# S5 matmuls in blocks of one array division, GLU in the S5 operand's token order, and a norm broadcast in two one-pass matmuls

## The chip, the cores and the metric

The kernel runs on one core of a Trainium2 chip. The metric is device time in microseconds (us): the median of several executions of the same program. Beside it stands one profiled execution, whose trace gives the start, the length and the waits of every instruction. PE is the matrix engine (TensorE), PEld its weight loads, DVE the vector engine, ACT the scalar engine, POOL the general one, and SPq and ACTq are the queues on which SyncE and ACT issue DMAs.

## The reference, cut to what matters

One decoder layer on 1056 tokens (a prompt of 1024 and 8 samples of 4), all in float32:

```
n = rmsnorm(h, g_in)
z_a, xbc, dt_raw, z_b, u_b = split(n @ w_in)
ya = ssd_branch(z_a, xbc, dt_raw, ...)       # conv, SiLU, chunked SSD scan, * SiLU(z_a), grouped norm
# s5_branch: 64 groups of 16 channels, each drives a complex diagonal state of 64
bu = einsum(u, bb);  x = scan(ab, bu)        # x_t = ab * x_(t-1) + bu_t
y = Re(einsum(x, c)) + s5_d * u
g = gelu(y)
y = g * sigmoid(g @ glu_w + glu_b)           # GLU
yb = y * silu(z_b)
h = h + concat(ya, yb) @ w_out
h = h + (p @ w_ple_proj) * sigmoid(rmsnorm(h, g_ple) @ w_ple_gate)
y_out = rmsnorm(h, g_final)
```

## The kernel before, in words

Every activation lies with channels on the 128 partitions and the 1056 tokens along a row. A float32 operand of a large product is split into a high and a low part of a one-pass type (`n_h`/`n_l`, `wh`/`wl`, `g_h`/`g_l`, `yb_h`/`yb_l`), and the product is taken as high·high + low·high + high·low. That is `dense` (L164, matmuls on L173): for a tile of 128 weight rows it goes through three chunks of 352 tokens, and in each through k = 0..7, three matmuls of 352 columns for each k, into one PSUM tile `psd`. Such dense tiles run through the whole kernel and make up most of its work: projections `u`, `z_b`, `z_a` and `xbc` (moving `n_h`/`n_l`), then GLU (moving `g_h`/`g_l`), the half of the output product that reads the S5 branch (WOB, moving `yb_h`/`yb_l`), the half that reads the SSD branch (WOA, moving `ya_h`/`ya_l`), and the gate.

The order of instructions on each engine is not written out by hand. The program is built under a scheduler that simulates a timeline and picks, on each engine, what comes next. So small matmuls of the S5 and SSD parts stand between dense matmuls of whatever weight tile is running. Buffers come from pools: 28 rows of one token row each, three PSUM tiles for `psd`, two of a pool A (`vr`, `vi`, `kp`, `nsp`, `xt`, `cb`) and three of a pool B (`wp`, `yp`, `nrb`, `yd`, `yo`, `st`).

The stages, in order of time:

- **First norm and the p projection.** A row's sum of squares is taken over partitions by small matmuls with a column of ones (`rstd_tok`, `nsp` L190), its inverse root is worked out on DVE in tiny tiles of 88 tokens x 12 (`nv`, `ny`, `nt`), and `rstd_bcast` (`nrb` L208) spreads it over the 128 partitions: four float32 matmuls per chunk, with the column `ny` broadcast as weights and an identity matrix as moving operand.
- **u projection with the S5 coefficients.** 16 calls of `s5_coef_batch`, one for four S5 groups. Each works out powers of the state matrix on DVE, then eight matmuls `kp` (L450, 64 rows by 32 columns of the array each), which ACT and DVE put into `ks`, and four transposes `wp` (L471, the whole array), copied into `wo`. Results go to DRAM tiles `kd`, `md` and `od`.
- **z_b and xbc projections with the S5 batches.** 16 calls of `s5_batch`, again four groups each. A batch loads `u8`, `mm` and `om` from DRAM; eight matmuls `vr`/`vi` (L642, 128 rows by 64 columns of the array) make the drive; DVE runs the scan and writes the states `sst`; eight matmuls `yp<-sst,om` (L688, 64 rows by 128 columns) and four `yp<-u,mm` (L684, the whole array) make y; ACT applies gelu and a DMA writes `gd`. `z_tile` (L597) makes z·(1+tanh(z/2)) out of a dense tile and stores it in `zb_d` or `za_d`.
- **SSD scan with the rest of z_a.** 16 units. Each needs a decay tile `ab`, loaded by a broadcasting DMA from `acs_d`, then eight relus, exp and a mask.
- **GLU.** `g_tile` loads gelu(y) from `gd` in its own order (step s of 8, then block c of 128 tokens) and splits it into `g_h` and `g_l`, written in token order. The eight GLU tiles follow; their evacuation loads `zb_d` as `gzl`, multiplies, and splits into `yb_h`/`yb_l`. `za_apply` multiplies the SSD output by `za_d` and sums its squares (`ysq`) on POOL. `ya_norm` (norm over 512 channels) follows GLU tiles 3 and 7.
- **WOB, WOA, gate and last norm.** WOB adds x and stores in `hp_d`; WOA adds `hp_d`; the gate stage multiplies; a last norm gives the output.

The loop that places the S5 batches among the other projections is this:

```
MID = "b0 c0 dt x0 z x1 z x2 x3 z b1 c1 z x4 x5 z x6 x7".split()
for nm in MID:
    ...                      # one dense tile: dt_tile(), z_next() or conv_tile(...)
    if nb < 16:
        s5_batch(nb)
        nb += 1
```

Of the kernel before, what the change touches and what calls it, by code (L numbers as in the profile page):

```python
# [7 lines left out]
F32 = mybir.dt.float32  # L8
F32R = mybir.dt.float32r
# [15 lines left out]
CW = 352  # L25
EPS = 1e-6
# [4 lines left out]
C_ID, C_CAUS, C_ONE, C_SMASK, C_BM, C_E8, C_I32, C_SAME, C_E16, C_N = 0, 128, 256, 384, 416, 424, 488, 520, 552, 568  # L31
# [3 lines left out]
def hymba_ssd_s5_kernel(  # L35
# [141 lines left out]

    nw_p = pool("nw", bufs=2)
# [4 lines left out]
    def rstd_tok(chunks, n, eps=EPS):  # L183
# [17 lines left out]
        return y  # L201

    def rstd_bcast(y):

        qt = y.shape[0]
# [30 lines left out]
    dma(out=cs, in_=cst)  # L236
    dma(out=vc, in_=vecs)
    dma(out=raws[1], in_=wall[M_PP + 1])
# [174 lines left out]
    def s5_coef_batch(b):  # L413
        cf2, P, Z = cfc["p2"], cfc["P"], cfc["Z"]
        g0, g1, j0 = GB * b, GB * b + GB, 2 * b
        if b % 4 == 0:
# [26 lines left out]
            in_=op[:, :, :, 1:9].rearrange("p j r k h -> p (j r) (k h)"))  # L443
        kp = psa("kp")[:, 0:128]
        for j in range(2):
            for ri in range(2):
                for q in range(2):
                    g, hq = 2 * j + q, slice(64 * q, 64 * q + 64)
                    o = 128 * ri + 32 * (b % 4) + 16 * j
                    PE.matmul(out=kp[32 * g:32 * g + 32], lhsT=cfc["zf"][hq, o:o + 32],  # L450
                              rhs=op[hq, j, ri, 0:8].rearrange("p k h -> p (k h)"), start=(ri == 0), stop=(ri == 1),
                              tile_position=(64 * q, 32 * g))
# [170 lines left out]
    def s5_batch(b):  # L623
# [15 lines left out]
        for g in range(NB):  # L639
            q, j = g % 2, g // 2  # L640
            for ri, v in ((0, vrv), (1, viv)):
                PE.matmul(out=v[64 * q:64 * q + 64, j], lhsT=wv[:, 2 * j + ri, 64 * q:64 * q + 64], rhs=u8[:, g, 8:144],  # L642
                          start=True, stop=True)
# [36 lines left out]
        yp = [psb("yp")[:, 0:136 * NJ].rearrange("p (j c) -> p j c", c=136) for _ in range(2)]  # L680
        for j in range(NJ):
            for q in range(2):
                g = 2 * j + q
                PE.matmul(out=yp[q][:, j], lhsT=tm[:, g], rhs=u8[:, g, 0:136], start=True, stop=False)  # L684
            for ri in range(2):
                for q in range(2):
                    hq = slice(64 * q, 64 * q + 64)
                    PE.matmul(out=yp[q][:, j], lhsT=om[hq, j, ri], rhs=sst[hq, ri, j, 0:136], start=False, stop=(ri == 1))  # L688
# [145 lines left out]
    def ya_norm(g):  # L834

        rt = rstd_tok([[ysq[c]] for c in range(3)], 512, 4 * EPS)
        for c in range(3):
            rs = rstd_bcast(rt[:, 4 * c:4 * c + 4])
# [59 lines left out]
    for nm in MID:  # L898
# [270 lines left out]
```

## Time and profile before

| | |
|---|---|
| median of three executions | 1076.1 us (1072.94 to 1078.46) |
| profiled execution: its own time | 1074.75 us |
| profiled execution: span, first to last instruction | 1072.8 us |
| mean granted PE clock | 0.988 |
| PE busy | 1036.2 us, 97% of the span, 6948 instructions |
| PEld busy | 964.9 us, 90% |
| DVE busy | 737.7 us, 69% |
| ACT busy | 425.4 us, 40% |
| POOL busy | 166.6 us, 16% |

Busy time is the union of an engine's instructions. PE's records overlap, since matmuls are pipelined: a matmul that is listed with 0.32 us starts some 0.16 us after the one before it, so it is the distance from start to start that tells what a matmul takes. The span is shorter than the execution's own time by 1.95 us, which lie ahead of the first and behind the last instruction. The granted clock is below 1 in four short stretches, 39.6 to 46.5, 234.2 to 237.6, 776.9 to 780.3 and from 1060.2 us on.

### The profile page before, as it was taken

What the parts mean: (1) busy time and instruction counts of PE and PEld (TensorE: products, weight loads), DVE (VectorE), ACT (ScalarE), POOL (GpSimd) and SP (SyncE); (2) the same over time, 40 slices, a digit from 0 to 9 for tenths busy, and PEclk for the clock granted to TensorE, in tenths of its full rate; (3) what the DMA queues carried; (4) which work ended last, traced back from release to release, by engine and by line L of the source; (5) the groups of instructions that cost most, each with busy time, mean ns of one, the idle gap of its engine ahead of it and who ended that gap; (6) DMA issues with size and microseconds to landing.
All of it is one profiled execution on the core that took longest, in us unless ns stands there. A gap on an engine that the chain in (4) does not pass through costs nothing.

```text
span 1072.8 us, 18551 instructions
## 1 busy us (share of the span) xinstructions
PE 1036.2 (97%) x6948; PEld 964.9 (90%) x6948; DVE 737.7 (69%) x1676; ACT 425.4 (40%) x861; POOL 166.6 (16%) x225
## 2 busy tenths in 40 slices
PE   7999999999999999999999997999999999999995
PEld 7899888889889999998878885899999999999995
DVE  5789989676888687545667579889862234445676
ACT  7533222444444334348644455443521023323321
POOL 0600000000000000021333223031300002221221
PEclk9899999999999999999999999999999999999997
DMA  9524577643444343343446656544444422321332
GB/s 319 184 83 139 167 226 226 192 148 105 136 162 164 111 163 109 105 143 101 166 177 209 199 157 177 161 136 124 126 136 151 139 98 87 107 97 62 115 108 101
DMA packets 120825, 156.02 MB, mean 145 GB/s; under 512 B 15776, under 2 KB 96800, under 8 KB 120736
## 3 DMA queue, kind: packets, MB, share of 16 engines
q1 hardware_dynamic: 91712, 135.31, 39.8%
q10 hardware_dynamic: 29024, 19.54, 5.8%
q8 instruction: 54, 0.88, 0.3%
q14 instruction: 35, 0.29, 0.1%
HBM read 108.34 MB, written 50.67 MB: 148 GB/s over the span
## 4 chain that ended last, share of the span: by engine, by line
PE 44%; DVE 4%; DMA 3%; ACT 2%; issue 2%; POOL 0%; SPq 0%; DVEq 0%; ACTq 0%; POOLq 0%
PE psd L173 37%; DMA ab<-acs_d 1%; PE nrb L208 1%; PE yd L712 1%; DVE g_l L73 1%; ACT ab L70 1%; PE yo L761 1%; PE st L764 1%; DMA gr<-gd 1%; PE nsp L190 1%; PE yq L812 1%; DMA ee<-eac_d 1%; PE xt L750 0%; ACT wh L70 0%; DVE x L73 0%
## 5 line engine op out<-in xcount | busy, mean ns | idle before, releaser
L173 PE MATMUL psd<-n_h,wh 128*128 128x352 f32 x864 | 285.9, 331 | 2.5 <-DVE zt L85 2.4
L173 PE MATMUL psd<-n_l,wh 128*128 128x352 f32 x864 | 284.9, 330 | 0.0
L173 PE MATMUL psd<-n_h,wl 128*128 128x352 f32 x864 | 282.3, 327 | 0.0
L173 PEld LDWEIGHTS psd<-n_h,wh 128*128 128x128 f32 x864 | 164.3, 190 | 11.8 <-issue 4.8
L173 PEld LDWEIGHTS psd<-n_l,wh 128*128 128x128 f32 x864 | 164.5, 190 | 2.6 <-issue 1.8
L173 PEld LDWEIGHTS psd<-n_h,wl 128*128 128x128 f32 x864 | 164.0, 190 | 2.7 <-issue 1.8
L73 DVE TENSOR_TENSOR wl<-wr,wh 128x1024 fp32r<-128x1024 f32 (+1 forms) x64 | 78.4, 1225 | 72.9 <-ACT wh L70 70.6
L70 ACT ACTIVATE wh<-wr 128x1024 fp32r<-128x1024 f32 (+1 forms) x65 | 67.0, 1031 | 145.6 <-PE psd L173 130.6
L173 PE MATMUL psd<-g_l,wh 128*128 128x352 f32 x192 | 62.6, 326 | 6.4 <-DVE g_l L73 6.4
L173 PE MATMUL psd<-g_h,wh 128*128 128x352 f32 x192 | 61.8, 328 | 3.2 <-ACT g_h L70 3.1
L173 PE MATMUL psd<-yb_l,wh 128*128 128x352 f32 x192 | 62.8, 327 | 0.0
L173 PE MATMUL psd<-yb_h,wl 128*128 128x352 f32 x192 | 62.5, 325 | 0.0
L173 PE MATMUL psd<-yb_h,wh 128*128 128x352 f32 x192 | 62.4, 326 | 0.0
L173 PE MATMUL psd<-ya_l,wh 128*128 128x352 f32 x192 | 61.8, 322 | 0.0
L173 PE MATMUL psd<-ya_h,wh 128*128 128x352 f32 x192 | 61.8, 322 | 0.0
L173 PE MATMUL psd<-g_h,wl 128*128 128x352 f32 x192 | 61.8, 322 | 0.0
L173 PE MATMUL psd<-ya_h,wl 128*128 128x352 f32 x192 | 61.8, 322 | 0.0
L70 ACT ACTIVATE ab<-ab,tok 128x128 f32<-128x128 f32 (+1 forms) x144 | 42.9, 381 | 44.8 <-DMA ab<-acs_d 25.4
L73 DVE TENSOR_TENSOR xl<-xl,psd 128x352 f32<-128x352 f32 x24 | 12.5, 520 | 52.0 <-PE psd L173 50.0
L173 PE MATMUL psd<-hg_h,gwh 128*128 128x400 f32 (+1 forms) x144 | 46.6, 323 | 0.0
L173 PE MATMUL psd<-hg_l,gwh 128*128 128x400 f32 (+1 forms) x144 | 46.6, 323 | 0.0
L73 POOL TENSOR_TENSOR ssq<-ssq,xl 128x352 f32<-128x352 f32 x21 | 21.2, 1008 | 162.4 <-DMA wr<-wall 105.7
(301 smaller groups left out, 2238.1 us busy)
## 6 DMA issues: line engine op xcount, KB each, us to landing
wr<-wall SPq DMA_DIRECT2D x68, 512.0 KB, 3.6
mm<-md SPq DMA_DIRECT2D x16, 512.0 KB, 4.8
ab<-acs_d SPq DMA_DIRECT2D x16, 512.0 KB, 5.0
ud<-ub ACTq DMA_DIRECT2D x8, 576.0 KB, 3.7
u<-ud SPq DMA_DIRECT2D x16, 288.0 KB, 3.3
gd<-yt SPq DMA_DIRECT2D x16, 272.0 KB, 4.8
gr<-gd SPq DMA_DIRECT2D x8, 544.0 KB, 4.3
x<-xT SPq DMA_DIRECT2D x24, 176.0 KB, 5.0
```

What stands on the lines that cost most here:

```text
L70: return S.activation(out=out, in_=in_, func=func, **kw)
L73: return (eng or V).tensor_tensor(out=out, in0=a, in1=b, op=op)
L173: PE.matmul(out=ps, lhsT=a[:, ko + k, :], rhs=b, start=(i == 0), stop=(i == 3 * K - 1))
L190: PE.matmul(out=sp[0:qt, 4 * c + j:4 * c + j + 1], lhsT=q[:, qt * j:qt * j + qt], rhs=ones[:, 0:1], start=(i == 0), stop=(i == len(sqs) - 1))
L208: PE.matmul(out=rb[:, qt * j:qt * j + qt], lhsT=y[:, j:j + 1].to_broadcast([qt, 128]), rhs=ident[0:qt, 0:qt], start=True, stop=True)
L712: PE.matmul(out=yd[64 * (e % 2):64 * (e % 2) + 64, e // 2], lhsT=x1[:, e], rhs=mt[:, e], start=True, stop=True)
L761: PE.matmul(out=yo[:, i], lhsT=hg[:, 128 * i:128 * i + 128], rhs=ct[g][:, cols], start=True, stop=True)
L764: PE.matmul(out=st, lhsT=bk, rhs=x2.rearrange("p e q -> p (e q)"), start=True, stop=True)
L812: PE.matmul(out=yq[q:q + 32], lhsT=cm[g][:, b], rhs=h_, start=(b < 2), stop=(b >= 6), tile_position=(0, q))
```

## The change

It has six parts.

- **Coefficient batches.** In `s5_coef_batch` the transposes `wp` are issued ahead of the `kp` matmuls, and all twelve stand in a chain (a new class `Chain`, which tells the scheduler to issue each directly after the one before).
- **S5 batches.** In `s5_batch` the `vi` and `vr` matmuls stand in one chain of eight, and the `yp` matmuls in one chain of twelve, the eight that read `sst` first, the four that read `u` behind them. The first batch comes one entry of `MID` later.
- **Token order.** `z_tile` stores `zb_d` in the order in which the S5 branch has its tokens (step s, then block c); `g_tile` writes `g_h`/`g_l` contiguously in that order; WOB's evacuation goes back to token order with a strided read of PSUM and a strided add, on a whole row of x loaded by one DMA, and stores the tile with one DMA.
- **GLU and WOB chunks.** 384, 384 and 288 tokens in place of 3 x 352; GLU tile 0 goes through k outermost, with its three PSUM tiles open at once (`dense_k`).
- **ya_norm(1)** moves from the end of GLU to behind WOB tile 0.
- **Norm broadcast.** `rstd_tok` splits `ny` into a high part `nyh` and a low part `nyl` of the one-pass type (a copy and a subtraction on DVE), and `rstd_bcast` takes two one-pass matmuls where one float32 matmul stood. The identity is kept in that type for this.

```
+PCH = ((0, 384), (384, 384), (768, 288))
...
+    def dense_k(w, rows_h, rows_l, evac, chunks):
+        hi, lo = w
+        pss = [ps_d.tile([128, 512], F32, tag="d", name="psd")[:, 0:n] for _, n in chunks]
+        for k in range(8):
+            for (t0, n), ps in zip(chunks, pss):
+                h, l = rows_h[k][:, t0:t0 + n], rows_l[k][:, t0:t0 + n]
+                for i, (a, b) in enumerate(((hi, h), (hi, l), (lo, h))):
+                    PE.matmul(out=ps, lhsT=a[:, k, :], rhs=b, start=(k == 0 and i == 0), stop=(k == 7 and i == 2))
...
 def rstd_tok
-        return y
+        yh, yl = (nw_p.tile([128, 12], F32R, tag=q, name=q, bufs=3)[0:qt, 0:w] for q in ("nyh", "nyl"))
+        V.tensor_copy(out=yh, in_=y)
+        sub(yl, y, yh)
+        return yh, yl
 def rstd_bcast
-            PE.matmul(out=rb[:, qt * j:qt * j + qt], lhsT=y[:, j:j + 1].to_broadcast([qt, 128]),
-                      rhs=ident[0:qt, 0:qt], start=True, stop=True)
+            for i, a in enumerate((yh, yl)):
+                PE.matmul(out=rb[:, qt * j:qt * j + qt], lhsT=a[:, j:j + 1].to_broadcast([qt, 128]),
+                          rhs=ident_r[0:qt, 0:qt], start=(i == 0), stop=(i == 1))
...
+    class Chain:
+        def __init__(self):
+            self.last = None
+        def __call__(self, f, *a, **kw):
+            if self.last is None:
+                self.last = f(*a, **kw)
+            else:
+                with tc.issue_after(self.last.ins):
+                    self.last = f(*a, **kw)
...
 def s5_coef_batch (wt is now worked out ahead of kp)
+        ch = Chain()
+        wp = psb("wp")
+        for i in (1, 3, 0, 2):
+            ch(PE.transpose, wp[:, 128 * i:128 * i + 128], wt[:, i // 2, i % 2].rearrange("p k h -> p (k h)"), ident)
         kp = psa("kp")[:, 0:128]
...
-                    PE.matmul(out=kp[32 * g:32 * g + 32], lhsT=cfc["zf"][hq, o:o + 32],
+                    ch(PE.matmul, out=kp[32 * g:32 * g + 32], lhsT=cfc["zf"][hq, o:o + 32],
...
 def z_tile, for j < 8
+            for a, b, d0, ns in ((0, nn, 0, 8),) + (((nn, n, NPT, 4),) if nn < n else ()):
+                v = t[:, a:b].rearrange("p (s c) -> p s c", s=ns)
+                pv = ps[:, a:b].rearrange("p (c s) -> p s c", s=ns)
+                act(v, pv, AF.Tanh, scale=0.5)
+                stt(v, v, 1.0, pv, ALU.add, ALU.mult)
...
+                dma(out=o[:, :, t0 // 8:t0 // 8 + nn // 8] if d0 == 0 else o, in_=v)
...
 def s5_batch
-        for g in range(NB):
-            q, j = g % 2, g // 2
-            for ri, v in ((0, vrv), (1, viv)):
-                PE.matmul(out=v[64 * q:64 * q + 64, j], ...)
+        ch = Chain()
+        for ri, v in ((1, viv), (0, vrv)):
+            for g in range(NB):
+                q, j = g % 2, g // 2
+                ch(PE.matmul, out=v[64 * q:64 * q + 64, j], ...)
...
+        ch = Chain()
         for j in range(NJ):
-            for q in range(2):
-                PE.matmul(out=yp[q][:, j], lhsT=tm[:, g], rhs=u8[:, g, 0:136], start=True, stop=False)
-            for ri in range(2):
+            for ri in (1, 0):
                 for q in range(2):
-                    PE.matmul(out=yp[q][:, j], lhsT=om[hq, j, ri], rhs=sst[hq, ri, j, 0:136], ...)
+                    ch(PE.matmul, out=yp[q][:, j], lhsT=om[hq, j, ri], rhs=sst[hq, ri, j, 0:136], ...)
+        for g in range(NB):
+            ch(PE.matmul, out=yp[g % 2][:, g // 2], lhsT=tm[:, g], rhs=u8[:, g, 0:136], ...)
...
-        if nb < 16:
+        if i > 0 and nb < 16:
             s5_batch(nb)
...
 def g_tile
-            v = lambda r: r[:, t0:t0 + n].rearrange("p (c s) -> p s c", s=s)
+            v = lambda r: r[:, t0:t0 + n].rearrange("p (s c) -> p s c", s=s)
...
-        if m % 4 == 3:
-            ya_norm(m // 4)
+        if m == 3:
+            ya_norm(0)
...
 WOB
+        x_ = row("xl")[:, 0:T]
+        dma(out=x_, in_=xT[m])
-            add(x_, x_, ps)
-            dma(out=hp_d[m, :, t0:t0 + n], in_=x_)
+                add(v, v, pv)
+            if c == 2:
+                dma(out=hp_d[m], in_=x_)
+        if m == 0:
+            ya_norm(1)
```

Where the scheduler puts these matmuls is shown at three places. PE's rows at one coefficient batch before, among dense matmuls of a u tile (a row is a line, the output and its operands, the shape of the output, and how many of it in a row):

```order
L173 MATMUL psd<-n_h_113,wh 128x352
L173 MATMUL psd<-n_l_121,wh 128x352
L173 MATMUL psd<-n_h_113,wl 128x352
L173 MATMUL psd<-n_h_114,wh 128x352
L450 MATMUL kp<-op,bz 32x128 x6
L471 MATMUL wp<-cs,wt 128x128 x3
L173 MATMUL psd<-n_l_122,wh 128x352
L173 MATMUL psd<-n_h_114,wl 128x352
L173 MATMUL psd<-n_h_115,wh 128x352
L173 MATMUL psd<-n_l_123,wh 128x352
L450 MATMUL kp<-op,bz 32x128 x2
L471 MATMUL wp<-cs,wt 128x128
```

And PE's rows at a coefficient batch of the changed kernel (L175 is its dense line, L238 the first instruction of a chain and L241 the others):

```order
L175 MATMUL psd<-n_h_112,wl 128x352
L175 MATMUL psd<-n_h_113,wh 128x352
L238 MATMUL wp<-ident_r,wt 128x128
L241 MATMUL wp<-ident_r,wt 128x128 x3
L241 MATMUL kp<-op,bz 32x128 x8
L175 MATMUL psd<-n_l_121,wh 128x352
L175 MATMUL psd<-n_h_113,wl 128x352
```

Two visits to a batch, each with two kinds of small matmul, have become one visit. PE's rows at an S5 batch before, late in the z_b and xbc projections, where the drive of one batch (`u_4334`) lies among the outputs of the batch ahead (`u_4167`):

```order
L642 MATMUL vr<-u_4334,mm 64x136
L642 MATMUL vi<-u_4334,mm 64x136
L642 MATMUL vr<-u_4334,mm 64x136
L688 MATMUL yp<-sst,om 128x136 x2
L642 MATMUL vr<-u_4334,mm 64x136
L642 MATMUL vi<-u_4334,mm 64x136
L642 MATMUL vr<-u_4334,mm 64x136
L688 MATMUL yp<-sst,om 128x136 x2
L684 MATMUL yp<-u_4167,mm 128x136 x2
L688 MATMUL yp<-sst,om 128x136 x4
L642 MATMUL vi<-u_4334,mm 64x136
L684 MATMUL yp<-u_4334,mm 128x136
```

PE's rows in the same part of the changed kernel, the drive of one batch and the outputs of the batch ahead of it:

```order
L175 MATMUL psd<-n_h_117,wl 128x352
L238 MATMUL vi<-u_4473,mm 64x136
L241 MATMUL vi<-u_4473,mm 64x136 x3
L241 MATMUL vr<-u_4473,mm 64x136 x4
L175 MATMUL psd<-n_h_110,wh 128x352
L175 MATMUL psd<-n_l_118,wh 128x352
L238 MATMUL yp<-sst,om 128x136
L241 MATMUL yp<-sst,om 128x136 x7
L241 MATMUL yp<-u_4307,mm 128x136 x4
L175 MATMUL psd<-n_h_110,wl 128x352
```

Each kind now stands together, and dense matmuls stand between the two chains. Over the whole program the times that a matmul follows one with another division of the array fall from 268 to 168. PE's rows at the second `ya_norm` before, among dense matmuls of WOB tile 0:

```order
L173 MATMUL psd<-yb_h_7450,wl 128x352
L173 MATMUL psd<-yb_h_7575,wh 128x352
L190 MATMUL nsp<-cs,ysq 88x1 x12
L173 MATMUL psd<-yb_l_7576,wh 128x352
L173 MATMUL psd<-yb_h_7575,wl 128x352
```

PE's rows there in the changed kernel, in the last chunk of WOB tile 0 and the first of tile 1:

```order
L175 MATMUL psd<-yb_h_8196,wl 128x288
L204 MATMUL nsp<-cs,ysq 88x1 x4
L175 MATMUL psd<-yb_h_7379,wh 128x384
L204 MATMUL nsp<-cs,ysq 88x1 x4
L175 MATMUL psd<-yb_h_8321,wh 128x288
L204 MATMUL nsp<-cs,ysq 88x1 x3
L175 MATMUL psd<-yb_l_8322,wh 128x288
```

The twelve `nsp` stood together behind 55 dense matmuls of WOB; now they stand in four pieces behind 69 to 73.

## Rows read from the trace of the kernel before

**Rows 1.** Busy time in stretches: stretch, length, each engine's busy (instructions), clock, DMA share, GB/s.
```profile
104.00:452.00 348.00, 347.44 (x2508) 309.39 (x2506) 275.15 (x700) 132.27 (x245) 17.95 (x72) 1.00 0.51 156
636.00:680.00 44.00, 33.46 (x224) 26.26 (x223) 40.72 (x60) 26.09 (x43) 11.90 (x7) 1.00 0.53 144
770.00:782.00 12.00, 10.32 (x66) 9.87 (x65) 7.37 (x23) 1.21 (x4) 5.64 (x3) 0.86 0.46 152
782.00:872.00 90.00, 90.00 (x571) 90.00 (x571) 33.15 (x56) 15.18 (x22) 0.00 (x0) 1.00 0.42 137
```

**Rows 2.** PE's timeline at one coefficient batch: start us, us, instruction.
```profile
123.95 0.32 PE L173 MATMUL psd<-n_h,wh 128*128 128x352 f32 x1
124.20 0.64 PE L450 MATMUL kp<-op,bz 64*32 64x128 f32 x12
124.78 0.55 PE L471 MATMUL wp<-cs,wt 128*128 128x128 f32 x3
125.08 0.41 PE L173 MATMUL psd<-n_l,wh 128*128 128x352 f32 x1
125.32 0.32 PE L173 MATMUL psd<-n_h,wl 128*128 128x352 f32 x1
...
125.65 0.32 PE L173 MATMUL psd<-n_l,wh 128*128 128x352 f32 x1
...
126.57 0.32 PE L173 MATMUL psd<-n_h,wh 128*128 128x352 f32 x1
```

**Rows 3.** PE's timeline, dense matmuls ahead of and behind a lone drive block.
```profile
222.64 0.32 PE L173 MATMUL psd<-n_h,wh 128*128 128x352 f32 x1
...
224.29 0.32 PE L173 MATMUL psd<-n_h,wl 128*128 128x352 f32 x1
```

**Rows 4.** PE's timeline at one S5 batch.
```profile
341.64 0.32 PE L173 MATMUL psd<-n_h,wl 128*128 128x352 f32 x1
...
343.78 0.50 PE L684 MATMUL yp<-u,mm 128*128 128x136 f32 x2
344.21 0.50 PE L688 MATMUL yp<-sst,om 64*128 64x136 f32 x4
344.64 0.73 PE L684 MATMUL yp<-u,mm 128*128 128x136 f32 x4
345.30 0.73 PE L688 MATMUL yp<-sst,om 64*128 64x136 f32 x8
345.97 0.43 PE L173 MATMUL psd<-n_h,wh 128*128 128x352 f32 x1
346.23 0.32 PE L173 MATMUL psd<-n_l,wh 128*128 128x352 f32 x1
```

**Rows 5.** Groups by line and shape: count, busy us, mean ns, idle before and releasers.
```profile
L73 DVE TENSOR_TENSOR wl<-wr,wh 128x1024 fp32r<-128x1024 f32 x62 | 77.0, 1242 | 71.3 <-ACT wh L70 69.0 <-DMA mm<-md 1.2 <-DMA om<-od 0.9
...
L73 DVE TENSOR_TENSOR g_l<-gr,g_h 128x1024 fp32r<-128x1024 f32 x8 | 17.6, 2195 | 0.2 <-ACT g_h L70 0.2
```

**Rows 6.** PE's timeline at the second `ya_norm`, with idle before and releaser.
```profile
773.65 0.79 PE L190 MATMUL nsp<-cs,ysq 128*88 128x1 f32 x8 [1.20 <-POOL ysq L73]
```

**Rows 7.** PE's timeline, last coefficient matmuls and first S5 drive.
```profile
198.96 0.64 PE L450 MATMUL kp<-op,bz 64*32 64x128 f32 x12
...
216.23 0.46 PE L642 MATMUL vr<-u,mm 128*64 128x136 f32 x4
```

**Rows 8.** ACT's and PE's timelines at the start of the SSD scan.
```profile
480.43 2.45 ACT L70 ACTIVATE ab<-ab,tok 128x128 f32<-128x128 f32 x8 [3.77 <-DMA ab<-acs_d]
...
491.35 0.43 PE L173 MATMUL psd<-n_h,wh 128*128 128x352 f32 x1 [2.44 <-DVE zt L85]
```

**Rows 9.** DMA issues: queue, count, KB each, median us from issue to landing.
```profile
ab<-acs_d SPq DMA_DIRECT2D x16, 512.0 KB, 5.0
```

**Rows 10.** Groups by line and shape of the norm, columns as in rows 5.
```profile
L208 PE MATMUL nrb<-cs,ny 88*128 88x88 f32 x96 | 12.3, 285 | 0.0
...
L85 DVE SCALAR_TENSOR_TENSOR nt<-ny,nt 88x4 f32<-88x4 f32 x9 | 2.8, 310 | 0.1
```

More of the change, by code (lines that the diff above doesn't have):

```diff
@@ L175, in dense @@
             evac(c, t0, n, ps)
+    def dense_k(w, rows_h, rows_l, evac, chunks):
[6 more added lines that the diff above has]
+                    PE.matmul(out=ps, lhsT=a[:, k, :], rhs=b, start=(k == 0 and i == 0), stop=(k == 7 and i == 2))
+        for c, (t0, n) in enumerate(chunks):
+            evac(c, t0, n, pss[c])
     nw_p = pool("nw", bufs=2)
@@ L235, in hymba_ssd_s5_kernel @@
         dma(out=xr[k][:, 0:CW], in_=xT[k, :, 0:CW])
-    dma(out=cs, in_=cst)
+    dma(out=cs, in_=cst[:, 0:C_ID])
+    idt = ev("idt", 128)
+    dma(out=idt, in_=cst[:, C_ID:C_N])
     dma(out=vc, in_=vecs)
+    V.tensor_copy(out=ident_r, in_=idt)
     dma(out=raws[1], in_=wall[M_PP + 1])
@@ L680, in s5_batch @@
         yp = [psb("yp")[:, 0:136 * NJ].rearrange("p (j c) -> p j c", c=136) for _ in range(2)]
+        ch = Chain()
         for j in range(NJ):
-            for q in range(2):
-                g = 2 * j + q
-                PE.matmul(out=yp[q][:, j], lhsT=tm[:, g], rhs=u8[:, g, 0:136], start=True, stop=False)
-            for ri in range(2):
+            for ri in (1, 0):
                 for q in range(2):
                     hq = slice(64 * q, 64 * q + 64)
-                    PE.matmul(out=yp[q][:, j], lhsT=om[hq, j, ri], rhs=sst[hq, ri, j, 0:136], start=False, stop=(ri == 1))
+                    ch(PE.matmul, out=yp[q][:, j], lhsT=om[hq, j, ri], rhs=sst[hq, ri, j, 0:136], start=(j == 0 and ri == 1),
+                       stop=False)
+        for g in range(NB):
+            ch(PE.matmul, out=yp[g % 2][:, g // 2], lhsT=tm[:, g], rhs=u8[:, g, 0:136], start=False, stop=(g >= NB - 2))
         for q in range(2):
@@ L837, in ya_norm @@
         for c in range(3):
-            rs = rstd_bcast(rt[:, 4 * c:4 * c + 4])
+            rs = rstd_bcast([r[:, 4 * c:4 * c + 4] for r in rt])
             for i in range(4):
@@ L897, in hymba_ssd_s5_kernel @@
     nb = 0
-    for nm in MID:
+    for i, nm in enumerate(MID):
         if nm == "dt":
@@ L970, in evac @@
             split(hi[:, t0:t0 + n], lo[:, t0:t0 + n], z)
-        dense(w, g_h, g_l, evac)
+        (dense_k if m == 0 else dense)(w, g_h, g_l, evac, chunks=PCH)
         yb_h.append(hi)
@@ L1022, in hymba_ssd_s5_kernel @@
     for c in range(3):
-        act(rs[:, CW * c:CW * c + CW], rstd_bcast(rt[:, 4 * c:4 * c + 4]))
+        act(rs[:, CW * c:CW * c + CW], rstd_bcast([r[:, 4 * c:4 * c + 4] for r in rt]))
     last, pend = [None], []
```

53 lines of the change are left out of this document (30 added, 23 removed).

## The prediction

> **What bounds the kernel now.** I read the page's busy shares first: PE is busy for 97% of the span, so a gain must either shorten what PE does or close one of its few gaps. Then the windows, for the stretches that the change touches [rows 1]. In the S5 stretch (104 to 452) PE is idle for 0.56 us in 348 and DVE for 72.85: PE is the limit there and DVE follows it with 79% of its time. In the 44 us around the start of GLU it is the other way round: PE is idle for 10.54 us and DVE busy for 40.72. In the last 12 us of GLU the clock falls to 0.86 on average. From 782 on PE has no gap at all for 90 us, and DVE is busy for 33. Then PE's timelines at single places [rows 2 to 4], where a start-to-start distance shows what each switch of the array's division costs, and at the waits where stages meet [rows 6 to 8].
>
> The unit is the dense step. Two steps take 125.32 to 125.65 [rows 2], 0.165 us each. A foreign block costs the distance between the dense starts around it, less its dense steps.
>
> **Coefficient batches.** Before, a batch is visited twice. The first visit (6 `kp`, 3 `wp`) runs from 123.95 to 125.32 with two dense steps in it: 1.37 − 0.33 = 1.04. The second (2 `kp`, 1 `wp`) from 125.65 to 126.57, again with two: 0.92 − 0.33 = 0.59. Together 1.63 [rows 2]. After, one visit does the work of both: 1.04, plus one more `wp` (three take 124.78 to 125.08, so 0.10), plus two more `kp`, four passes (twelve take 0.58, so 0.19, of which I take 0.15 since part of the 0.58 is the entry). That is 1.29, a gain of 0.34, and 5.4 over 16 batches. A chain waits for its last operand, and `wt` and `op` of one batch are made one behind the other on DVE, so I take **4.5** (2.5 if half the visits lose something, 6 if the entry is cheaper too).
>
> **S5 batches.** Before, one batch runs from 341.64 to 345.97 + one dense step. From 341.64 to 346.23 are 4.59 us with two dense steps, so 4.26; one `u` matmul of the batch lies elsewhere, 0.23 with its share of a switch (an estimate from two in 0.43 [rows 4]). That makes 4.49, with eight changes of division. After, two visits. The drive chain is like the lone one at 222.64: 1.65 to the next plain dense start with two steps in it, 1.32 [rows 3]. For the output chain: 0.09 to enter (the dense step ahead of a block is 0.25 instead of 0.165 [rows 2]); 16 passes on `sst`, of which four take 0.43 and eight 0.67 [rows 4], so 0.67 + 8 x 0.06 = 1.15; eight passes on `u`, two in 0.43 and four in 0.66, so 0.115 for each further one: 0.66 + 4 x 0.115 − 0.10 = 1.02, the 0.10 because dense follows in the same division. Together 2.26, with the drive 3.58. The gain is 0.91 a batch, **14.6** over 16. Bounds: 11, if chains of half the batches are split or late, and 16, if the entries cost nothing.
>
> The first dense matmul after a switch steps by 0.26 where others step by 0.165 [rows 4]: 0.10 more, for a weight load in the one-pass type that nothing covers, and that is as long as a whole float32 `wp` (0.10). The Trainium skill, TensorE: Matmul & The Clock Gate, section Weight-path perf modes, says that the fast weight load is on where 128 weights are loaded and the type isn't float32. By it the one-pass loads of the norm's broadcast would be short too, and the sum would come out some 7 us lower, at 1043.5 (a rival below); the row rather speaks against it.
>
> **Start of GLU.** `g_l` is subtracted with a stride of eight at 2195 ns for 1056 columns, the unstrided `wl` of 1024 at 1242 [rows 5]. Written contiguously, `g_l` should fall by 0.95 us, eight times 7.6. PE is idle for 10.54 us in this stretch and DVE nearly full [rows 1], so nearly all of it counts: **7**. Bounds 3 (if the load of `gr` or ACT's part is late next, ACT being busy for 26 of 44) and 10.5 (all of the idle time). `dense_k` changes little: PE's order there was already k by k over three chunks.
>
> **The second ya_norm.** Before, PE waits 1.20 us for POOL's sum [rows 6], and the clock over those 12 us is 0.86 [rows 1], so 12 x 0.14 = 1.7 are lost to it as well: PE had been idle in that stretch before the clock fell. After, the `nsp` stand 14 dense steps later, 2.3 us, which is more than the wait. 1.2 + 1.7 = 2.9, taken as **2.5** (1 to 3). What reads the result (`ya_split` behind WOB 0) has the whole of WOB as cover.
>
> **Start of S5.** The first batch needs what the last coefficient batches stored. Before, 198.96 to 216.23 lie between, 17.3 us [rows 7]. After, 86 dense matmuls stand there, 14.2, and the rest of a `kp` chain, 0.7: 14.9. If all of the 17.3 were needed, PE waits 2.4. How much of it was needed no row shows: taken **−1.5** (0 to −2.4, and some 1.7 more if the clock falls as in the stretch above).
>
> **Start of SSD.** PE waited 2.44 us at 491.35, and ACT 3.77 for the first `ab` [rows 8]. After, the outputs of the last S5 batch come later among the projections: 104 dense matmuls (17.2 us) lie between the last `yp` and the first `yd`. In that time must pass the store of `gd` (taken like `ab`), the load of `ab`, whose storage the S5 pools hold until then (5.0 [rows 9]), and two times eight relus (2.45 each), which ACT now does in one go: 5 + 5 + 4.9 = 14.9, and gelu, exp and the mask besides. So it may come out even or late: taken **−2** (from +2.4, the wait gone, to −5).
>
> **Norm.** Two more tiny DVE operations, at 0.31 each [rows 10], lie on PE's path at about two of the norms, the first and the last: with their latencies, some **−0.9** in all (0 to −1.2; elsewhere dense work covers them). The passes of `nrb` stay as many: 96 of 88 columns take 12.3 us, 0.128 each [rows 10], 120 of this kind in all. One-pass ones are in no row: at the pace of dense, 0.165, they cost 4.4 more, at that of a `sst` pass, 0.06, they save 8. I take 0, since 0.128 lies between.
>
> **Costed at nothing.** The strided product of `zt`: at 0.43 us each (1242 x 352/1024) and dearer by 2195/1242 it adds 0.33, for 24 chunks 7.9 us on DVE, against 72.85 idle. Its scattered stores of `zb_d` are read from 680 on. WOB's strided add: DVE is busy for 33 of 90 us [rows 1]. Chunks of 384 and 288 move the same columns.
>
> **The sum.** 4.5 + 14.6 + 7 + 2.5 − 1.5 − 2 − 0.9 = 24.2. Against the profiled execution's 1074.75 that gives **1050.5**. That execution lies 1.35 us below the median, well within the spread of the three.
>
> **Rivals.**
>
> *DVE is late.* With 19 us less on PE, the S5 stretch is 329 long and DVE needs 275 + 7.9 of it, 86%. That is an average: late in the stretch the next chain may wait for `sst` instead of running piece by piece, as before. If half of 19.1 goes, the time is 1060. For it: chains need everything at once. Against: two dense matmuls between the chains can be many, and PE had 0.56 us of gaps.
>
> *One-pass broadcast is faster, or the stage starts cost nothing.* By the lower bound above `nrb` saves up to 8, say 7, so 1043.5; without the waits at the starts 3.5 less give 1047. The Trainium skill's rule on the fast weight load (the page and section above) would have this come about.
>
> *Slower: a chain stalls PE at its head.* A chain that is scheduled before its `sst` is there stops PE, and all dense work behind it. The gain is 24.2, or 1.5 us for each of 16 batches: a stall of more than 1.5 a batch decides it, and at 2 the time is 1082. For it: PE works strictly in order and the scheduler places chains by a simulated time. Against: before, the same `sst` was awaited by the same scheduler and PE was idle for 0.56 us in 348 [rows 1].
>
> *The change does not do what it says.* If the switches cost nothing, or the blocks take as long whole as in pieces, only small gains and the starts' losses are left: about 1070 to 1074. Against: rows 2 and 4 show the step after a switch.
>
> **How the numbers follow.** The forecast 0.69; DVE late 0.14; faster broadcast or no waits 0.09; no effect 0.03; stalls 0.05. A difference of 0.5% (5.4 us) is about what a measurement of this kernel can tell from none. Faster: 0.69 + 0.14 + 0.09 = 0.92; same 0.03; slower 0.05. The range leaves out the last two and the far ends of the bounds: 1064 takes in DVE late with half of GLU's gain gone, 1038 the faster broadcast together with the upper bounds of coefficients, S5 and GLU (1050.5 − 7 − 1.5 − 1.4 − 2.6).
>
> **What would show it.** In the changed trace: one visit of about 1.3 us for each coefficient batch; in the S5 stretch two visits of 1.3 and 2.3, PE without gaps, and some 19 us less from 104 to 452; `g_l` near 1.25 us and PE's idle time at the start of GLU near 3.5; no wait at the second `nsp`, and a clock of 1.00 there; waits of 1 to 2 us at the first `vi` and around the first `yd`. Wrong would be: gaps on PE at the heads of chains, `g_l` fast but PE as idle (then the load of `gr` or ACT was the limit), or `nrb` steps far from 0.128.

## The result, and the profile after

The changed kernel took 1045.54 us (median of four, 1042.21 to 1046.2) against 1077.28 us for the kernel before (median of four, 1072.94 to 1079.22), measured beside it: a ratio of 0.9705, with a 95% interval of 0.9667 to 0.9742. The profiled execution took 1046.13 us against 1074.75, so 28.6 less, where 24.2 had been forecast.

Both kernels run 5040 dense matmuls, 72 for each tile of weights, and the tiles in the same order. So the start of the n-th dense matmul in one trace, less that in the other, tells at the borders of the tiles how far the changed kernel is ahead (numbers count from 0):

| at the dense matmul (number) | before, us | after, us | ahead, us |
|---|---|---|---|
| in the u projection, ahead of the coefficients (504) | 102.32 | 102.93 | −0.6 |
| behind the coefficients (936) | 196.79 | 191.28 | 5.5 |
| late in the projections (2016) | 456.88 | 432.58 | 24.3 |
| start of the SSD scan (2232) | 498.07 | 477.11 | 21.0 |
| in the SSD scan (2448) | 563.88 | 539.72 | 24.2 |
| first of GLU (2736) | 642.94 | 618.33 | 24.6 |
| GLU tile 1 (2880) | 689.97 | 660.56 | 29.4 |
| first of WOB (3312) | 763.46 | 734.14 | 29.3 |
| WOB tile 1 (3456) | 794.97 | 766.29 | 28.7 |
| gate (4896) | 1037.88 | 1009.23 | 28.7 |

The small matmuls don't stand at the same places among the dense ones in both kernels. At 2016 the changed kernel has its last output chain still before it, and at 2232 it has two units' `yd` behind it where the kernel before has one, so part of 24.3 and 21.0 is only that; at 2448 both have done the same work.

The windows of the changed kernel for the stretches of [rows 1], moved by what it is ahead (the columns are the same):

```profile
100.00:428.00 328.00, 326.65 (x2507) 305.26 (x2507) 266.54 (x684) 132.36 (x252) 18.00 (x72) 1.00 0.57 164
611.40:655.40 44.00, 38.90 (x254) 33.20 (x253) 39.00 (x70) 19.24 (x42) 8.91 (x7) 0.96 0.63 171
741.00:753.00 12.00, 10.94 (x69) 10.85 (x68) 9.75 (x23) 2.99 (x5) 3.00 (x3) 0.79 0.32 125
753.00:843.00 90.00, 90.00 (x566) 90.00 (x565) 40.33 (x68) 13.77 (x21) 0.00 (x0) 0.99 0.33 116
```

The S5 stretch holds the same matmuls (2507 against 2508) in 328 us where 348 were needed, and PE still has hardly a gap (1.35 us): the work on PE itself has become shorter. PE's idle time around the start of GLU has halved, 5.1 us of 44. The third row has not got better: the clock there is 0.79 now.

PE's timeline of one coefficient batch after, which answers to [rows 2]:

```profile
123.34 0.32 PE L175 MATMUL psd<-n_h,wh 128*128 128x352 f32 x1
123.50 0.27 PE L238 MATMUL wp<-ident_r,wt 128*128 128x128 f32 x1
123.61 0.49 PE L241 MATMUL wp<-ident_r,wt 128*128 128x128 f32 x3
124.02 0.64 PE L241 MATMUL kp<-op,bz 64*32 64x128 f32 x16
124.59 0.43 PE L175 MATMUL psd<-n_l,wh 128*128 128x352 f32 x1
124.86 0.32 PE L175 MATMUL psd<-n_h,wl 128*128 128x352 f32 x1
```

From 123.34 to 124.86 less two dense steps are 1.19 us; the two visits before were 1.63. PE's timeline of an S5 drive and, right behind it, of an output chain, which answers to [rows 3, 4]:

```profile
323.81 0.32 PE L175 MATMUL psd<-n_h,wl 128*128 128x352 f32 x1
...
325.40 0.32 PE L175 MATMUL psd<-n_l,wh 128*128 128x352 f32 x1
325.66 0.38 PE L238 MATMUL yp<-sst,om 64*128 64x136 f32 x1
...
326.79 1.19 PE L241 MATMUL yp<-u,mm 128*128 128x136 f32 x8
327.73 0.41 PE L175 MATMUL psd<-n_h,wl 128*128 128x352 f32 x1
327.98 0.32 PE L175 MATMUL psd<-n_h,wh 128*128 128x352 f32 x1
```

The drive takes 1.26 (forecast 1.32), the output chain 2.25 (forecast 2.26). At the start of WOB, PE's, DVE's and ACT's timelines show what took the place of [rows 6]:

```profile
747.91 0.51 PE L175 MATMUL psd<-yb_h,wh 128*128 128x288 f32 x1 [1.06 <-ACT yb_h L71]
```

```profile
736.73 2.70 DVE L74 TENSOR_TENSOR ya_l<-x,ya_h 128x352 fp32r<-128x352 f32 x6
...
746.95 0.44 DVE L86 SCALAR_TENSOR_TENSOR gzl<-gzl,zt 128x288 f32<-128x288 f32 x1
```

```profile
747.42 0.44 ACT L71 ACTIVATE yb_h<-gzl 128x288 fp32r<-128x288 f32 x1 [1.74 <-DVE gzl L86]
```

PE no longer waits for POOL's sum but for `yb_h`, the last part of GLU, and that for a product on DVE, whose queue holds splits of `ya` ahead of it. Behind this wait the clock stands at half (1.2 of 2.4 GHz) for 6.8 us, from 748.0 to 754.9. At the start of GLU the subtraction of `g_l` has become short, and one of the waits that are left there is for `g_h`:

```profile
L74 DVE TENSOR_TENSOR g_l<-gr,g_h 128x1024 fp32r<-128x1024 f32 x8 | 10.1, 1268 | 1.6 <-ACT g_h L71 1.6
```

```profile
628.11 0.87 PE L187 MATMUL psd<-g_h,wh 128*128 128x384 f32 x3 [1.31 <-ACT g_h L71]
```

Behind that wait the clock stands at half from 628.6 to 632.0.

### The profile page after: what moved, and what is told of

It is laid out like the page before. It is cut to its first block, busy times and chain, and to the rows that moved or that the text cites. A ratio compares the mean times of both kernels' runs of the same rounds, so it can differ in the third digit from the quotient of the medians.

```text
span 1044.1 us, 18506 instructions
## 1 busy us (share of the span) xinstructions
PE 1010.2 (97%) x6948; PEld 958.1 (92%) x6948; DVE 742.3 (71%) x1711; ACT 420.2 (40%) x869; POOL 154.0 (15%) x225
## 4 chain that ended last, share of the span: by engine, by line
PE 83%; DVE 7%; DMA 5%; ACT 3%; issue 1%; SPq 0%; ACTq 0%; DVEq 0%
PE psd L175 68%; PE yp L241 3%; DVE x L86 1%; DMA wr<-wall 1%; PE yd L761 1%; PE nrb L227 1%; ACT ab L71 1%; DMA ab<-acs_d 1%; PE yo L810 1%; DMA gr<-gd 1%; PE kp L241 1%; PE st L813 1%; PE psd L568 1%; PE nsp L204 1%; PE vr L241 1%
## 5 line engine op out<-in xcount | busy, mean ns | idle before, releaser
L175 PE MATMUL psd<-n_h,wh 128*128 128x352 f32 x864 | 283.8, 329 | 1.4 <-ACT n_h L71 1.0
L175 PE MATMUL psd<-n_l,wh 128*128 128x352 f32 x864 | 282.9, 327 | 2.3 <-DVE n_l L74 2.3
L175 PE MATMUL psd<-n_h,wl 128*128 128x352 f32 x864 | 281.1, 326 | 0.1
L175 PEld LDWEIGHTS psd<-n_h,wh 128*128 128x128 f32 x864 | 162.9, 189 | 11.7 <-issue 6.2
L175 PEld LDWEIGHTS psd<-n_l,wh 128*128 128x128 f32 x864 | 163.1, 189 | 6.8 <-issue 4.0
L175 PEld LDWEIGHTS psd<-n_h,wl 128*128 128x128 f32 x864 | 163.0, 189 | 2.5 <-issue 1.9
L175 PE MATMUL psd<-yb_h,wh 128*128 128x384 f32 (+1 forms) x192 | 63.0, 329 | 1.1 <-ACT yb_h L71 1.1
L175 PE MATMUL psd<-yb_l,wh 128*128 128x384 f32 (+1 forms) x192 | 63.4, 330 | 0.0
L175 PE MATMUL psd<-yb_h,wl 128*128 128x384 f32 (+1 forms) x192 | 62.9, 328 | 0.0
L175 PE MATMUL psd<-ya_h,wh 128*128 128x352 f32 x192 | 61.8, 322 | 0.0
L175 PE MATMUL psd<-ya_l,wh 128*128 128x352 f32 x192 | 61.8, 322 | 0.0
L175 PE MATMUL psd<-ya_h,wl 128*128 128x352 f32 x192 | 61.8, 322 | 0.0
L74 DVE TENSOR_TENSOR xl<-xl,psd 128x384 f32<-128x384 f32 (+2 forms) x32 | 21.4, 695 | 46.0 <-PE psd L175 46.0
L175 PE MATMUL psd<-g_h,wh 128*128 128x384 f32 (+1 forms) x168 | 54.0, 321 | 0.1
L175 PE MATMUL psd<-g_h,wl 128*128 128x384 f32 (+1 forms) x168 | 54.0, 322 | 0.0
L175 PE MATMUL psd<-g_l,wh 128*128 128x384 f32 (+1 forms) x168 | 54.0, 321 | 0.0
L175 PE MATMUL psd<-hg_h,gwh 128*128 128x400 f32 (+1 forms) x144 | 46.6, 324 | 0.0
L175 PE MATMUL psd<-hg_l,gwh 128*128 128x400 f32 (+1 forms) x144 | 46.5, 323 | 0.0
L175 PE MATMUL psd<-hg_h,gwl 128*128 128x400 f32 (+1 forms) x144 | 46.3, 323 | 0.0
```

The source lines that it names most:

```text
L74: return (eng or V).tensor_tensor(out=out, in0=a, in1=b, op=op)
L175: PE.matmul(out=ps, lhsT=a[:, ko + k, :], rhs=b, start=(i == 0), stop=(i == 3 * K - 1))
```

## The experiments

All comparisons "ahead" are made as in the table, at the same dense matmul of two traces. The kernel before, timed beside each set of runs, had medians from 1073.35 to 1077.62, so a difference of a few us between two medians of different sets says little by itself; where the argument is about so little, it rests on the traces.

**The S5 matmuls without chains.** The order of code is that of before, for `vr`/`vi` and `yp`.

```
-        ch = Chain()
-        for ri, v in ((1, viv), (0, vrv)):
-            for g in range(NB): ...  ch(PE.matmul, ...)
+        for g in range(NB):
+            for ri, v in ((0, vrv), (1, viv)):  ...  PE.matmul(...)
...            (and yp: for each j, two u, then four sst)
```

> The changed kernel with the S5 matmuls issued as before (drive and output matmuls in the old order, no chains); all else as changed. Theory A (what counts is how often PE changes the array's division): the order on PE shows 62 more changes than the changed kernel, a batch goes from 3.53 us (1.28 + 2.26) back to about 4.5, so the time rises by 13 to 17 us, to 1059 to 1063. Rival B (the gain in this stretch comes from fewer waits or from the clock, not from the blocks): less than 5 us.

It took 1060.51 us, ratio 0.9873 (0.9837 to 0.9909) to before. The trace falls behind the changed kernel only while S5 batches run: from 1.2 us ahead to 12.2 behind, 13.4 in all, at 62 changes of division more. A is right.

**The coefficients without chains.**

```
-        wt = ...; cmul(wt ...)            # ahead of kp
-        ch(PE.transpose, wp ...) x4;  ch(PE.matmul, kp ...) x8
+        PE.matmul(kp ...) x8;  ks ...
+        wt = ...; cmul(wt ...);  PE.transpose(wp ...) x4
```

> The changed kernel with the coefficient batches issued as before (kp ahead of wt, no chain). Theory A: 32 more changes of division; a batch takes 1.65 us in two visits where the changed kernel's one visit takes 1.21, so 16 x 0.44 = 7 us more, 1052 to 1053. Rival B (DVE, 89% busy in this stage, sets its length anyway): under 2 us.

1048.87 us, ratio 0.9771 (0.9735 to 0.9807). Within the coefficient stage the trace loses 7.6 us to the changed kernel (from 0.9 ahead to 6.7 behind at 936). It wins 1.7 back at the first S5 drive, where PE doesn't wait in this run, and 1.9 at the start of GLU, where the clock stays whole. The size is A's in that stage. The final time, 3.3 more, is under A's 1052 to 1053 and could not have told it, being within the spread of the runs.

**Divisions by turns, in one visit.**

```
         for j in range(NJ):
             for ri in (1, 0):
                 for q in range(2):  ...  ch(PE.matmul, out=yp[q][:, j], lhsT=om[hq, j, ri], ...)
-        for g in range(NB):
-            ch(PE.matmul, out=yp[g % 2][:, g // 2], lhsT=tm[:, g], ...)
+                g = 2 * j + 1 - ri
+                ch(PE.matmul, out=yp[g % 2][:, g // 2], lhsT=tm[:, g], ...)
```

> The changed kernel with the output chain in another order: two sst matmuls and one u matmul by turns, four times, still one chain and one visit, same work. Theory A: 6 more changes of division in each batch. From the groups of before, a group of sst passes costs 0.19 us beside its passes and a group of u passes 0.20, so three more of each are 1.17 us a batch, 18.7 us in all: 1061 to 1067. Rival C (a visit costs, whatever is in it, since it is the entry from dense and the way back): no change, 1045.

1063.98 us, ratio 0.9906 (0.9879 to 0.9933). PE's timeline of one output chain:

```profile
334.65 0.32 PE L175 MATMUL psd<-n_h,wh 128*128 128x352 f32 x1
...
335.34 0.50 PE L241 MATMUL yp<-u,mm 128*128 128x136 f32 x2
335.77 0.50 PE L241 MATMUL yp<-sst,om 64*128 64x136 f32 x4
...
338.18 0.41 PE L175 MATMUL psd<-n_l,wh 128*128 128x352 f32 x1
338.42 0.32 PE L175 MATMUL psd<-n_h,wl 128*128 128x352 f32 x1
```

The chain takes 3.77 − 0.33 = 3.44 us instead of 2.25, with the same passes: six more changes cost 1.19, 0.20 each, and 19 us over 16 batches. The whole run is 18.4 slower. This decides between A and C: a visit costs by its changes of division, not by being a visit. What a change spends its 0.20 us on, no run separates.

**The chains alone, on the kernel before.** The edit is the two chains of the diff, with the order of matmuls in them, and nothing else.

> The kernel before with the two chains alone (coefficients and S5), first S5 batch as before, no other part of the change. Theory A: 7 us from the coefficients and 15.5 from S5 are independent of the rest: 1077 - 22.5 = 1053 to 1056, and PE's dense matmuls run as far ahead of before at the end of the S5 stage as in the changed kernel. Rival D (the late first batch and the other parts were needed for the blocks to pay): less than 15 us gained.

1050.84 us, ratio 0.9793 (0.9757 to 0.9829), a little better than A's 1053 to 1056. It is 23 to 23.5 us ahead of before at the end of the S5 stage and stays there to the end. So 23.5 of the 28.6 us come with the chains, and all the rest of the change together brings some 5. Of the 23.5, 1.7 are the half-clock stretch that the trace of before has at 234 and none of the other traces has.

**The norm's broadcast as before.**

```
-            for i, a in enumerate((yh, yl)):
-                PE.matmul(out=rb[...], lhsT=a[:, j:j + 1].to_broadcast([qt, 128]), ...)
+            PE.matmul(out=rb[...], lhsT=y[:, j:j + 1].to_broadcast([qt, 128]), ...)
```

> The changed kernel with the norm's broadcast as before (one float32 matmul for each quarter, no high and low part), all else as changed. Theory A: a pass of the broadcast takes the same in either type (0.11 us from start to start in both traces at full clock), and only the two small DVE operations at exposed places go: the last norm is 0.2 us shorter from the last nsp to the end of the span, the time within 1.5 us of the changed kernel's 1045.5. Rival B (one-pass passes are loaded faster): 5 to 8 us slower, and a nrb step near 0.19 us.

1044.24 us, ratio 0.969 (0.9673 to 0.9707). PE's timeline of the changed kernel has the one-pass broadcasts 0.11 apart; that of the kernel before has eight float32 passes and the next dense matmul:

```profile
42.93 0.29 PE L227 MATMUL nrb<-ident_r,nyh 88*128 88x88 f32 x1
43.04 0.29 PE L227 MATMUL nrb<-ident_r,nyl 88*128 88x88 f32 x1
43.16 0.29 PE L227 MATMUL nrb<-ident_r,nyh 88*128 88x88 f32 x1
```

```profile
53.98 1.02 PE L208 MATMUL nrb<-cs,ny 88*128 88x88 f32 x8
54.80 0.41 PE L173 MATMUL psd<-n_h,wl 128*128 128x352 f32 x1
```

0.82 us for eight are 0.10 each: the one-pass type is no faster here. What the Trainium skill says (TensorE: Matmul & The Clock Gate, Weight-path perf modes) of the fast weight load for types other than float32 does not show in these loads. A is right: in the time this part of the change is worth nothing that can be measured. Its price shows once: at the last norm PE waits 2.34 us for the inverse root in this run and in the kernel before, and 2.53 in the changed kernel, 0.19 for the two small operations.

**The second ya_norm back at the end of GLU.**

```
-        if m == 3:
-            ya_norm(0)
+        if m % 4 == 3:
+            ya_norm(m // 4)
...
-        if m == 0:
-            ya_norm(1)
```

> The changed kernel with the second ya_norm back at the end of GLU. In the changed kernel PE waits there 1.06 us for yb_h, the last high part of GLU, and the clock then stands at half for some 6.6 us (before: 1.20 us for POOL's sum, 3.4 us at half). Theory A (the wait has passed from POOL's sum to the last GLU evacuation, which stands behind the splits of the SSD half in DVE's queue): PE waits about as long with the norm back, and the time differs by less than 2 us either way. Rival B (the move is worth its 2.5 us): 1048.

1042.92 us, ratio 0.9673 (0.9657 to 0.9689). In its trace PE does not wait there, the clock falls for 3.4 us (748.9 to 752.3) instead of 6.8, and from WOB tile 0 to tile 1 it gains 2.3 us on the changed kernel. Neither theory has it: B has the sign wrong, and A had said a wait of about the same length. ACT's and PE's timelines show why no wait is left:

```profile
747.32 0.44 ACT L71 ACTIVATE yb_h<-gzl 128x288 fp32r<-128x288 f32 x1 [1.78 <-DVE gzl L86]
```

```profile
746.42 1.34 PE L204 MATMUL nsp<-cs,ysq 128*88 128x1 f32 x16
747.82 0.40 PE L175 MATMUL psd<-yb_h,wh 128*128 128x288 f32 x1
```

The last part of GLU is as late as in the changed kernel (747.32 against 747.42), but here `nsp` fill the time in which PE sat idle there. And the clock fell without a wait of PE ahead of it that is longer than 0.25 us.

**The splits of the SSD half held back.**

```
+            glu_end[0] = split(hi[:, t0:t0 + n], lo[:, t0:t0 + n], z)
...
-        ya_split(m)
+        with tc.issue_after(glu_end[0].ins):
+            ya_split(m)
```

> The changed kernel with the splits of the SSD half (ya_h, ya_l) held back until the last GLU evacuation has ended; the second ya_norm stays behind WOB tile 0. Theory A (in the changed kernel DVE works on nine ya_l splits, 4 us, ahead of the last GLU evacuation, and so makes PE wait 1.06 us for yb_h and the clock fall): that wait is gone, the clock stays whole or falls for less than 3.5 us, and PE is 1.5 to 3 us earlier in WOB tile 1 than in the changed kernel. Rival B (the pieces of nsp between the dense matmuls cause it): wait and clock as in the changed kernel.

One run, 1042.32 us. ACT's timeline at the last part of GLU, PE's at the `nsp`, and the window of 13 us around it:

```profile
743.87 0.44 ACT L71 ACTIVATE yb_h<-gzl 128x288 fp32r<-128x288 f32 x1 [1.89 <-DVE gzl L86]
```

```profile
746.58 1.97 PE L204 MATMUL nsp<-cs,ysq 128*88 128x1 f32 x24
```

```profile
738.00:751.00 13.00, 13.00 (x95) 13.00 (x95) 12.49 (x23) 6.51 (x15) 3.26 (x3) 1.00 0.57 208
```

No wait, the clock whole, and 4.4 us gained from WOB tile 0 to tile 1, more than the 1.5 to 3 expected: 1.06 of them the wait, 3.4 of them half of the 6.8 us that the changed kernel spends at half clock. With the splits out of its way `yb_h` is 3.5 us earlier than in the changed kernel, and the wait is gone: on the wait A is right, and the place of the `nsp` behind WOB tile 0 did not cause it. But the `nsp` stand in one piece in this run and in four in the changed kernel, so for the clock B is not excluded: with the second ya_norm back at the end of GLU the wait was gone too, the `nsp` stood in two pieces, and the clock fell all the same.

**The token order of before.** `z_tile`, `g_tile`, GLU's and WOB's chunks and WOB's evacuation as before, all else as changed.

```
-            v = lambda r: r[:, t0:t0 + n].rearrange("p (s c) -> p s c", s=s)
+            v = lambda r: r[:, t0:t0 + n].rearrange("p (c s) -> p s c", s=s)
...
-        (dense_k if m == 0 else dense)(w, g_h, g_l, evac, chunks=PCH)
+        dense(w, g_h, g_l, evac)
```

> The changed kernel with the token order as before: z_b stored in token order, g_h and g_l written with a stride, three chunks of 352, WOB's evacuation by chunks; the chains, the late first batch, the move of ya_norm and the norm's broadcast stay. Theory A (the strided subtraction was on PE's path at the start of GLU): the start of GLU loses 4.8 us against the changed kernel, g_l is back near 2.2 us, 1049 to 1051. Rival B (the chunks of 384 and the k-outermost tile gave the gain): the same time, but it would also show as g_l being slow without PE idling longer; rival C (WOB's slower strided add costs as much as GLU gains): 1045.

1053.14 us, ratio 0.9767 (0.9744 to 0.9789): 7.6 more than the changed kernel. The group of the strided subtraction and PE's timeline in GLU tile 0:

```profile
L74 DVE TENSOR_TENSOR g_l<-gr,g_h 128x1024 fp32r<-128x1024 f32 x8 | 17.6, 2200 | 0.1
```

```profile
646.80 0.66 PE L175 MATMUL psd<-g_l,wh 128*128 128x352 f32 x1 [3.18 <-DVE g_l L74]
```

It falls 7.5 us behind from 2592 to 2880, around the start of GLU, part of it by two falls of the clock, and 0.6 more by the end. In all PE waits 4.5 us for `g_l` in this run and 0.8 in the changed kernel. A is right on the place and on PE's wait for `g_l`; its size was too small. The run also puts back the three equal chunks and the order of GLU tile 0, and what these do by themselves it does not separate. C is out: nothing is won back at WOB.

**GLU's input not loaded.**

```
-        dma(out=gr, in_=gd[:, 2 * j:2 * j + 2].rearrange("t h g c -> (h g) t c"))
+        G.memset(gr, 0.25)
```

> The changed kernel with the eight loads of gr (gelu of y, out of gd) left out: POOL fills the buffer with a constant instead, so this leaves out the data of the GLU input. Theory A (after the subtraction has become short, the loads of gr through two buffers are what PE waits for at the start of GLU): PE's idle time from the last 44 us around the start of GLU, 5.1 us in the changed kernel, falls under 2 us, and GLU tile 0 ends 3 to 5 us earlier. Rival B (ACT's and DVE's work for the SSD units is the limit there): idle time stays at 4 us or more.

One run, 1039.5 us. The window around the start of GLU (that of the changed kernel moved by the 2.0 us that this run is ahead there), and ACT's timeline of the changed kernel, where `g_h` waits for its load:

```profile
609.40:653.40 44.00, 41.09 (x285) 36.67 (x285) 42.43 (x78) 21.62 (x48) 19.22 (x13) 1.00 0.37 110
```

```profile
636.51 1.18 ACT L71 ACTIVATE g_h<-gr 128x1024 fp32r<-128x1024 f32 x2 [2.48 <-DMA gr<-gd]
...
645.21 1.18 ACT L71 ACTIVATE g_h<-gr 128x1024 fp32r<-128x1024 f32 x2 [5.06 <-DMA gr<-gd]
```

PE's idle time falls from 5.1 to 2.9 us and the clock stays whole; GLU tile 1 comes 4.3 us earlier. So the loads were next, as A says, but not down to the 2 us that it gave: DVE is busy for 42.4 of 44, and the two long waits that are left, 1.04 us of `yd` for `yt` and 1.50 for `g_l`, both end on DVE. That is B's part.

**The first S5 batch at the first entry.**

```
-        if i > 0 and nb < 16:
+        if nb < 16:
```

> The changed kernel with the first S5 batch at the first entry, as before, instead of one entry later. Theory A (the first batch's data is late only if the batch comes early; behind 86 dense matmuls the changed kernel waits 1.0 us for its u): with the batch at the first entry PE's dense work ends the S5 stage within 1 us of the changed kernel, since a batch that waits lets dense matmuls pass ahead. Rival B (the placing is worth more than a microsecond): 1 to 3 us more at the first drive, by a wait there or by the clock behind it.

One run, 1048.59 us. PE's timeline at the second drive:

```profile
205.72 0.46 PE L238 MATMUL vi<-u,mm 128*64 128x136 f32 x1 [3.02 <-DVE a4h L74]
```

The first drive waits 0.29 us (0.98 in the changed kernel), but the second then stops PE for 3.02 until DVE has used the first batch's `vi`, and the clock falls to a mean of 0.66 from 203 to 213. By matmul 2160, with all S5 batches through in both kernels, it has lost 4.5 us to the changed kernel, and 4.6 remain at the end. A is wrong and B right in kind, with a larger price and at the second drive.

**Loading GLU's input into its own row,** with the second ya_norm back at the end of GLU; and the same with the splits held back.

```
+        if j >= 2:
+            l32 = lo.bitcast(F32)
+            dma(out=l32[:, 0:NPT] ..., in_=src[:, :, 8:136])
+            dma(out=l32[:, NPT:T] ..., in_=src[:, 0:4, 0:8])
+            for t0, t1 in ((0, NPT), (NPT, T)):
+                split(hi[:, t0:t1], lo[:, t0:t1], l32[:, t0:t1])
```

> The changed kernel with the second ya_norm back at the end of GLU, and six of the eight GLU input tiles loaded straight into the row that becomes g_l, so that they don't pass through the two buffers of gr. Theory A (those two buffers are what PE waits for at the start of GLU; without any load the stretch was 4.3 us shorter): 2 to 4 us less than with the norm back alone (1042.9), 1039 to 1041. Rival B (the rows come free so late that the loads start no earlier): 1043 or more.

> The same with the splits of the SSD half held back as well. Theory A: the splits in DVE's queue cost 0 to 2 us where the norm is at the end of GLU, since no wait for yb_h was left there: 1038 to 1041, within 2 us of the kernel without holding them back. Rival B (splits that come late are late for WOA or for WOB's evacuations): slower by 1 us or more.

1044.25 us, ratio 0.9715 (0.9685 to 0.9745), and 1040.88 us, ratio 0.968 (0.9644 to 0.9715). The start of GLU is shorter by 2.6 and 1.5 us than in the changed kernel, but the two lose 4.6 and 3.5 again at the first ya_norm, where PE now waits 0.3 to 0.7 us for POOL's sum at each of its chunks and the clock falls for 6.8 and 3.4 us. The second version has the lowest median of all kernels that do the whole work, 4.7 under the changed kernel, but the intervals of the ratios overlap. The first ended in B's range and the second in A's, and neither for its reason: the gain at GLU is there and is gone one stage later. That the direct loads cause this later loss is not shown: the run with the norm's broadcast as before, which loads as the changed kernel does, loses 3.7 us at the same place, with a wait of 0.32 us and a clock at half from 692.7 to 699.5.

## Why the prediction was right

The forecast was 1050.5 us with a range of 1038 to 1064; the median is 5 us under it. The mechanism of the two large terms, fewer changes of the array's division, is shown by the runs with and without chains. That the whole came so near is in part luck: GLU and the second ya_norm brought 5.3 us less than forecast, and the coefficients, the start of SSD and a stretch of half clock that no term had brought 7.5 more.

**What bounds it.** Right: the S5 stretch was PE's own work, so shortening the work shortened the stretch, and PE stayed without gaps.

**Coefficients.** Forecast 4.5, measured 7: a block takes 1.19 us instead of the 1.29 of the sum, 0.44 less than the two visits of before, and all 16 are whole. (The table has 6.1 by matmul 936, where the kernel before still has one visit to make.) The discount for late DVE work was not needed.

**S5 batches.** Forecast 14.6. Both visits measured within 0.06 us of the forecast. Summed over the traces, the visits of the S5 matmuls take 71.5 us before and 56.5 after, without the waits in them: 15.0. With the 7 of the coefficients and the 1.7 of half clock at 234 that is about the 23.5 of the run with the chains alone.

**Start of S5.** Forecast −1.5: PE waits 0.98 us for `u`. The half-clock stretch of before at 234 is gone, some 1.7 us (half of 3.4), which no term had.

**Start of SSD.** Forecast −2. ACT waits 3.16 us for `ab` and then does 16 relus at a stretch, as the term has it, but PE is not stopped by it: between 2160 and 2232 it is idle for 1.10 us, where it was 2.44 before. So 1.3 were gained where 2 were taken as lost; the sign is wrong, within the term's bounds. The 3.3 us by which the table falls from 2016 to 2232 are small matmuls that stand earlier, and are back at 2448.

**Start of GLU.** Forecast 7, gained 4.8, with PE idle for 5.1 us where 3.5 were expected. `g_l` fell as forecast, from 2195 to 1268 ns. What was missed is the fall of the clock at 628.6 to 632 behind a wait of 1.31 us (1.7 us lost), and the loads of `gr`, named as the lower bound, which came next.

**The second ya_norm.** The term that failed outright: forecast 2.5 gained, measured 0.6 lost. The step "14 dense steps later, 2.3 us, which is more than the wait" looked at POOL's sum alone. The last evacuation of GLU stood behind splits in DVE's queue and was late next; with the norm back at the end of GLU `nsp` cover that time. With the splits held back 4.4 us come back.

**Norm.** Forecast −0.9: the changed kernel is 0.6 behind ahead of the coefficients. Its third part ran with DVE doing 15 products in a row, and PE waited 2.27 us for `n_l`; but kernels that have this part as the changed kernel has it differ from it by up to 2.1 us there, so its cause stays open. At the last norm the two operations cost 0.19 us, not the 0.45 of the term, and `nrb` steps by 0.11 us where it stepped by 0.10.

**The rivals.** DVE late and stalls at chain heads did not happen; PE's idle time in the stretch is 1.35 us, of which 0.98 are the first drive. That they can happen shows in the run with the first batch an entry earlier, where the head of a chain stops PE for 3.02 us. The faster broadcast is refuted. In the range's lower end the upper bound of GLU should stand as 3.5 (10.5 − 7) and not 2.6, which moves that end to 1037; nothing hangs on it.

## What to carry to other kernels

Count how often PE changes the division of its array and price each change from the timeline: here 0.20 us, and 100 of them were 2% of the kernel. A block of 8 or 12 small matmuls, sorted by division, paid for two changes of division here, whether it held one kind of small matmul or two. Where a wait is removed, read in the queues of all engines what arrives next at the same place. Look at the clock behind each wait as well: a wait of 1.06 us stood here ahead of a stretch at half clock that cost 3.4 more.

## What the runs showed of the hardware

In two places of the changed kernel, between the first norm and the last, the granted clock fell to half behind a wait of PE: from 748.0 to 754.9 behind 1.06 us, and from 628.6 to 632.0 behind 1.31. In both the time lost to the clock (half of the stretch, 3.4 and 1.7 us) is longer than the wait. But a wait of this length does not decide it. In the run with the splits held back PE waited 1.14 us at 628.60 and 1.63 at 641.32, and the clock stayed whole from 55 us to the last norm; in the run with the second ya_norm at the end of GLU it fell at 748.9 without a wait of over 0.25 us ahead of it, and in the kernel before at 234.2 likewise. What brings a fall about is not shown here.

Six changes of division cost 1.19 us with all else the same, 0.20 each. A change into the whole array costs about as much as one out of it: in the run by turns a group of two `u` passes and a group of four `sst` passes both take 0.43 us from start to start, 0.20 and 0.19 beside their passes.
